# The gates of a bidirectional gated recurrence, computed as 64-row tiles with both gates of a head side by side

## The chip, the cores and the metric

One core of a Trainium2 chip runs the whole program. The metric is device time in microseconds; three runs of the kernel before give the median. Engines are named as in the profile: PE is TensorE (PEld its weight loads), ACT is ScalarE, DVE is VectorE, POOL is GpSimd, SP is SyncE, which issues the DMAs.

## The reference

A trunk of two layers over 1024 latent and 256 context tokens of width 1024. Layer 0 runs a bidirectional gated recurrence (RG-LRU) over 512 channels in 8 heads of 64 beside a spatial gating unit; layer 1 runs a short convolution beside differential attention. The change lies in the recurrence's gates. Per direction:

```python
def rglru_coeffs(xc, w_a, b_a, w_x, b_x, lam):
    xh = xc.reshape(bsz, n, LRU_HEADS, LRU_HEAD_DIM)          # 8 heads of 64
    gate_r = jax.nn.sigmoid(jnp.einsum('blhi,hij->blhj', xh, w_a).reshape(bsz, n, BRANCH_WIDTH) + b_a)
    gate_i = jax.nn.sigmoid(jnp.einsum('blhi,hij->blhj', xh, w_x).reshape(bsz, n, BRANCH_WIDTH) + b_x)
    log_a = (-LRU_C * gate_r.astype(jnp.float32)) * jax.nn.softplus(-lam.astype(jnp.float32))
    a = jnp.exp(log_a)
    bterm = jnp.sqrt(-jnp.expm1(2.0 * log_a)) * (gate_i * xc).astype(jnp.float32)
    return a, bterm
```

The gates of a head depend on that head's 64 channels alone. The scan h = a h + bterm then runs forward and backward over the tokens.

## The kernel before

Channels lie on the partitions, tokens along the free axis. The 512 channels of the recurrence are four feature blocks f of 128, two heads each; 256 context and 1024 latent tokens make 1282 columns with a gap of two. Precision comes from splitting each fp32 value into a high and a low part of a shorter format (`split`: ScalarE copies the high part, another engine subtracts), so each product is three matmuls: high by high, high by low, low by high.

Per block, `lru_x(f)` projects the channels (tile px), copies them out of PSUM on ScalarE (xp, L353 and L354), convolves them on VectorE (xl) and splits them into xh and xo. `lru_g(f)` projects the branch gate (tile pg). `lru_rec(f)` computes the recurrence's gates. For each direction d and each of the two gates g it runs nine matmuls over three chunks of columns (258, 512, 512) into a tile pgate. The two heads of a block stand as a block diagonal in a 128 x 128 weight, half of it zeros. ScalarE evicts a gate with one tanh of 128 x 1282 (L393; sigmoid is taken from tanh), to gr and gx; then tt and exp (L397, L398), products on VectorE, and in `lru_scan` a sqrt on ScalarE (L411) and the scans on VectorE. The order in the program is x(1), rec(0), scan(0), g(1), x(2), rec(1) and so on; behind rec(3) the spatial gating unit starts with the projection pz and with v (tile pv, weights wvr split into wvh on ScalarE and wvl on GpSimd).

`mod_step()` puts a piece of work of another kind, the modulation of layer 1, between the matmuls: four small matmuls in column tiles (modp), transposes (modcp) or one matmul with two outputs (gatep).

px, pg, pu, pz, pv and pgate all come from one pool of PSUM, pj, with two buffers of three banks that go round:

```python
    def pj3(name):
        t = pj.tile([128, 1536], F32, name=name, tag="pj", bufs=2)
        return t
```

TensorE's order is the program's. The order on the other engines is set by the framework's scheduler when the program is built, and each engine then runs its list in order.

Of the kernel before, what the change touches and what calls it, by code (L numbers as in the profile page):

```python
# [10 lines left out]
F32 = mybir.dt.float32  # L11
F32R = mybir.dt.float32r
# [18 lines left out]
    ("cc", 16), ("bmod0", 24), ("bmod1", 24), ("convw", 16), ("convb", 4), ("ba", 8), ("bx", 8), ("lam", 8),  # L31
# [11 lines left out]
def tile_hybrid_trunk(es: ExitStack, tc: tile.TileContext, A, out, scr=None):  # L43
# [40 lines left out]
    def P(k):  # L84
        o, w = POFF[k]
        return par[:, o:o + w]
# [11 lines left out]
    hb = const.tile([128, 16], F32, name="hb")  # L98
    V.tensor_scalar(hb[:, 0:8], P("ba"), 0.5, None, op0=ALU.mult)
    V.tensor_scalar(hb[:, 8:16], P("bx"), 0.5, None, op0=ALU.mult)  # L100
# [42 lines left out]
    def wload(src, nk=8, le=None):  # L143
        raw = wp.tile([128, nk, 128], F32, name="wraw", tag="wraw", bufs=2)
        SY.dma_start(raw, src)
        res = []
        for h in range(nk // 4):
            hi = wp.tile([128, 4, 128], F32R, name="whi", tag="whi", bufs=4)
            lo = wp.tile([128, 4, 128], F32R, name="wlo", tag="wlo", bufs=4)
            split(hi, lo, raw[:, 4 * h:4 * h + 4], le=le or G)  # L150
            res.append((hi, lo))
        return res

# [96 lines left out]
# [3 lines that stand above are left out]
# [81 lines left out]
    lru_cm = ExitStack()  # L334
    lb, ld = lru_cm.enter_context(pool("lrub")), lru_cm.enter_context(pool("lrud"))
    with pool("lrua") as lp, pool("lruc") as lc:
        def lt(name, tag, bufs, dt=F32):
            t = {"gr": lb, "gx": lb, "tt": lb, "xl": lc}.get(tag, lp).tile([128, WC], dt, name=name, tag=tag, bufs=bufs)
            return t
# [36 lines left out]
        def lru_rec(f):  # L376
            (wh, wl), = wload(A["wg"][f], nk=4)
# [3 lines left out]
            for d in range(2):  # L381
                i8 = 4 * d + f
                gts = []
                for g in range(2):
                    p = pj3("pgate")
                    m = 2 * d + g
                    for c0, n in ((0, 258), (258, 512), (770, 512)):
                        o = p[:, 254 + c0:254 + c0 + n]
                        T.matmul(o, wh[:, m], xh[:, c0:c0 + n], start=True, stop=False)
                        T.matmul(o, wh[:, m], xo[:, c0:c0 + n], start=False, stop=False)  # L390
                        T.matmul(o, wl[:, m], xh[:, c0:c0 + n], start=False, stop=True)
                    t = lt("gt", "gr" if g == 0 else "gx", 2)
                    S.activation(t, p[:, 254:1536], AF.Tanh, scale=0.5, bias=hb[:, 8 * g + i8:8 * g + i8 + 1])  # L393
                    gts.append(t)
                r, gi = gts
# [751 lines left out]
def pack(inputs):  # L1147
# [8 lines left out]
    def cols(v):  # L1156
        v = np.asarray(v)
        return v.reshape(-1, 128).T
# [6 lines left out]
        "ba": cols(a["lru_b_a"][0]), "bx": cols(a["lru_b_x"][0]), "lam": cols(a["lru_lambda"][0]),  # L1165
# [22 lines left out]
    wg = np.zeros((4, 128, 4, 128), f)  # L1188
    for fi in range(4):
        for d in range(2):  # L1190
            for g, nm in enumerate(("lru_w_a", "lru_w_x")):
                for s in range(2):
                    wg[fi, 64 * s:64 * s + 64, 2 * d + g, 64 * s:64 * s + 64] = a[nm][0, d, 2 * fi + s]
# [30 lines left out]
```

## Time and profile before

| | us |
|---|---|
| median of 3 runs | 1170.76 (1170.17 to 1171.86) |
| profiled execution, span from first to last instruction | 1170.5 |
| PE busy | 1132.6 (97%) |
| DVE busy | 738.9 (63%) |
| ACT busy | 440.2 (38%) |
| POOL busy | 329.6 (28%) |

The time of the profiled execution is its span, 1170.5 us; it lies within the three runs. Busy times are sums over the whole program, whose stages have different limits. A matmul's end is modelled, so that the time from start to start says what one costs. The recurrence's gates lie between 73 and 208 us.

### The profile page before, as it was taken

The numbers are of one execution on the slowest core, as the hardware profiler recorded it, in microseconds if no ns is written. First come the engines' busy times: TensorE is split into PE (matmuls) and PEld (weight loads), VectorE is DVE, ScalarE is ACT, GpSimd is POOL, SyncE is SP. The second block draws the span as 40 slices with busy tenths as digits, with TensorE's granted clock in tenths as the row PEclk, the third lists the DMA queues.
The fourth block names the chain that finished last, engine by engine and source line by source line (L and its number), as shares of the span: only waits on it lengthen the run. The fifth ranks groups of instructions, "written<-read, shape, count | busy, mean of one in ns | idle before, by whom it ended". The sixth has DMA issues, their size and how long they took to land.

```text
span 1170.5 us, 14967 instructions
## 1 busy us (share of the span) xinstructions
PE 1132.6 (97%) x5842; PEld 922.0 (79%) x5842; DVE 738.9 (63%) x1007; ACT 440.2 (38%) x685; POOL 329.6 (28%) x200
## 2 busy tenths in 40 slices
PE   6999999899999999999999899999999999999997
PEld 3667777678888888888887788788888788888776
DVE  5677986943411475636104668876777877738897
ACT  3453654621121234342113455544544554413110
POOL 1114212620240132258104311221121321221971
PEclk9999999999999999999999999999999999999999
DMA  9654551230332444243215411322221510126622
GB/s 373 239 182 142 180 176 41 73 130 1 120 104 71 144 139 147 96 136 140 77 45 162 113 55 54 95 76 84 77 76 37 146 62 19 46 72 249 218 99 82
DMA packets 71606, 133.93 MB, mean 114 GB/s; under 512 B 6368, under 2 KB 34912, under 8 KB 70640
## 3 DMA queue, kind: packets, MB, share of 16 engines
q1 hardware_dynamic: 71536, 132.97, 34.3%
q8 instruction: 46, 0.75, 0.3%
q14 instruction: 24, 0.20, 0.1%
HBM read 105.67 MB, written 27.28 MB: 114 GB/s over the span
## 4 chain that ended last, share of the span: by engine, by line
PE 83%; DVE 8%; DMA 3%; ACT 3%; issue 2%; POOL 0%; SPq 0%; POOLq 0%; DVEq 0%; ACTq 0%
PE px L164 5%; PE pu L164 5%; PE pg L164 5%; PE p L174 5%; PE p L175 5%; PE p L176 5%; PE pout L648 4%; PE pout L646 4%; PE pout L647 4%; PE pz L164 4%; PE psc L942 3%; PE pv L198 3%; PE pv L199 3%; PE pv L200 3%; PE psc L943 3%; PE atr L965 3%
## 5 line engine op out<-in xcount | busy, mean ns | idle before, releaser
L141 POOL TENSOR_TENSOR wlo<-wraw,whi 128x512 fp32r<-128x512 f32 x92 | 148.1, 1615 | 458.5 <-ACT whi L138 449.8
L648 PE MATMUL pout<-woh,ylo 128*128 128x512 f32 (+1 forms) x296 | 114.5, 387 | 3.1 <-DVE ylo L141 3.1
L946 ACT ACTIVATE e<-psc,st 128x1280 f32<-128x1280 f32 x64 | 85.1, 1329 | 85.6 <-DVE st L944 85.6
L646 PE MATMUL pout<-woh,yhi 128*128 128x512 f32 (+1 forms) x296 | 114.8, 388 | 0.2
L647 PE MATMUL pout<-wol,yhi 128*128 128x512 f32 (+1 forms) x296 | 114.0, 385 | 0.0
L944 DVE TENSOR_REDUCE st<-psc 128x1 f32<-128x1280 f32 x64 | 95.0, 1485 | 27.8 <-PE psc L943 27.7
L138 ACT ACTIVATE whi<-wraw 128x512 fp32r<-128x512 f32 x92 | 57.2, 628 | 134.3 <-PE p L175 27.7
L174 PE MATMUL p<-hhl,whi 128*128 128x512 f32 x256 | 106.8, 417 | 0.0
L176 PE MATMUL p<-hhl,wlo 128*128 128x512 f32 x256 | 100.7, 393 | 0.0
L175 PE MATMUL p<-hll,whi 128*128 128x512 f32 x256 | 100.5, 393 | 0.0
L942 PE MATMUL psc<-k,qh 128*128 128x512 f32 (+1 forms) x192 | 68.0, 369 | 8.4 <-ACT e L946 8.4
L943 PE MATMUL psc<-k,ql 128*128 128x512 f32 (+1 forms) x192 | 69.3, 361 | 0.0
L138 ACT ACTIVATE ah<-atr 128x512 fp32r<-128x512 f32 (+1 forms) x96 | 48.5, 525 | 51.6 <-PE atr L965 50.6
L648 PEld LDWEIGHTS pout<-woh,ylo 128*128 128x128 f32 x296 | 55.6, 188 | 15.3 <-DVE ylo L141 4.0
L646 PEld LDWEIGHTS pout<-woh,yhi 128*128 128x128 f32 x296 | 55.6, 188 | 12.1 <-DVE zt L610 0.5
L647 PEld LDWEIGHTS pout<-wol,yhi 128*128 128x128 f32 x296 | 55.7, 188 | 11.5
L138 ACT ACTIVATE yhi<-yraw 128x512 fp32r<-128x512 f32 x36 | 22.5, 630 | 103.7 <-PE pout L647 57.6
L141 DVE TENSOR_TENSOR al<-atr,ah 128x512 fp32r<-128x512 f32 (+1 forms) x96 | 55.6, 594 | 5.8 <-ACT ah L138 5.6
L176 PEld LDWEIGHTS p<-hhl,wlo 128*128 128x128 f32 x256 | 48.2, 188 | 10.7
L175 PEld LDWEIGHTS p<-hll,whi 128*128 128x128 f32 x256 | 48.6, 190 | 7.3
L141 DVE TENSOR_TENSOR ylo<-yraw,yhi 128x512 fp32r<-128x512 f32 x36 | 43.2, 1208 | 17.5 <-ACT yhi L138 17.5
L174 PEld LDWEIGHTS p<-hhl,whi 128*128 128x128 f32 x256 | 48.4, 189 | 7.2
(292 smaller groups left out, 2822.2 us busy)
## 6 DMA issues: line engine op xcount, KB each, us to landing
wraw<-in_w_in_dram SPq DMA_DIRECT2D x44, 512.0 KB, 3.7
wm<-in_w_mod_dram SPq DMA_DIRECT2D x64, 256.0 KB, 3.4
wraw<-in_w_out_dram SPq DMA_DIRECT2D x16, 512.0 KB, 3.5
wm<-in_w_mod_dram SPq DMA_DIRECT2D x7, 1024.0 KB
xt<-in_xcT_dram SPq DMA_DIRECT2D x8, 640.0 KB, 9.8
xres<-in_xc_dram SPq DMA_DIRECT2D x10, 512.0 KB, 3.7
kd<-k_d SPq DMA_DIRECT2D x16, 320.0 KB, 4.7
wvr<-in_w_v_dram SPq DMA_DIRECT2D x8, 512.0 KB, 4.4
```

What stands on the lines that cost most here:

```text
L138: S.activation(hi, src, AF.Copy)
L141: le.tensor_tensor(lo, src, f32(hi), op=ALU.subtract)
L164: T.matmul(o, wt[:, k % 4], hh[hx][:, k], start=st, stop=sp_)
L174: T.matmul(o, hi[:, k % 4], hh[:, k], start=k == 0, stop=False)
L175: T.matmul(o, hi[:, k % 4], hl_[:, k], start=False, stop=False)
L176: T.matmul(o, lo[:, k % 4], hh[:, k], start=False, stop=k == KT - 1)
L646: T.matmul(o, hi[:, i], wh[:, c], start=first and i == 0, stop=False)
L647: T.matmul(o, hi[:, i], wl[:, c], start=False, stop=False)
L648: T.matmul(o, lo[:, i], wh[:, c], start=False, stop=not first and i == 3)
L942: T.matmul(o, qh[:, m, cu], KS[m][:, c:c + n], start=True, stop=False)
L943: T.matmul(o, ql[:, m, cu], KS[m][:, c:c + n], start=False, stop=True)
L944: V.tensor_reduce(st[:, m:m + 1], p[:, 256:1536], axis=AX.X, op=ALU.max, negate=True)
```

## The change

The weights of the gates are packed anew: for each direction, head 0's 64 rows stand in the upper half and head 1's in the lower, and the 128 columns are both gates of that head (64 columns each). The block diagonal's zeros are gone, and the load is half as large (`gload`). Each matmul takes 64 rows, in the upper or the lower half of the array (`tile_position`), and the two halves' matmuls alternate. Each head has its own tile pgate, both gates in it. The tanh has to bring the lanes back into the order of the channels: four activations of 64 x 1282, one for each gate and head, in place of two of 128 x 1282. The biases are packed the same way (hg).

```diff
-    hb = const.tile([128, 16], F32, name="hb")
-    V.tensor_scalar(hb[:, 0:8], P("ba"), 0.5, None, op0=ALU.mult)
-    V.tensor_scalar(hb[:, 8:16], P("bx"), 0.5, None, op0=ALU.mult)
+    hg = const.tile([128, 16], F32, name="hg")
+    V.tensor_scalar(hg, P("bg"), 0.5, None, op0=ALU.mult)
...
+    def gload(src):
+        raw = wp.tile([128, 2, 128], F32, name="wraw", tag="wraw", bufs=2)
+        SY.dma_start(raw, src)
+        hi = wp.tile([128, 2, 128], F32R, name="whi", tag="whi", bufs=4)
+        lo = wp.tile([128, 2, 128], F32R, name="wlo", tag="wlo", bufs=4)
+        split(hi, lo, raw, le=G)
+        return (hi, lo),
...
         def lru_rec(f):
-            (wh, wl), = wload(A["wg"][f], nk=4)
+            (wh, wl), = gload(A["wg"][f])
             mod_step()
             xl, xh, xo = XL[f]
             bs = []
             for d in range(2):
                 i8 = 4 * d + f
-                gts = []
-                for g in range(2):
-                    p = pj3("pgate")
-                    m = 2 * d + g
-                    for c0, n in ((0, 258), (258, 512), (770, 512)):
-                        o = p[:, 254 + c0:254 + c0 + n]
-                        T.matmul(o, wh[:, m], xh[:, c0:c0 + n], start=True, stop=False)
-                        T.matmul(o, wh[:, m], xo[:, c0:c0 + n], start=False, stop=False)
-                        T.matmul(o, wl[:, m], xh[:, c0:c0 + n], start=False, stop=True)
-                    t = lt("gt", "gr" if g == 0 else "gx", 2)
-                    S.activation(t, p[:, 254:1536], AF.Tanh, scale=0.5, bias=hb[:, 8 * g + i8:8 * g + i8 + 1])
-                    gts.append(t)
-                r, gi = gts
+                ps = [pj3("pgate"), pj3("pgate")]
+                for c0, n in ((0, 258), (258, 512), (770, 512)):
+                    for wt, x, st, sp_ in ((wh, xh, True, False), (wh, xo, False, False), (wl, xh, False, True)):
+                        for h in range(2):
+                            r64 = slice(64 * h, 64 * h + 64)
+                            T.matmul(ps[h][:, 254 + c0:254 + c0 + n], wt[r64, d], x[r64, c0:c0 + n], start=st,
+                                     stop=sp_, tile_position=(64 * h, 0))
+                r, gi = lt("gt", "gr", 2), lt("gt", "gx", 2)
+                for g, t in enumerate((r, gi)):
+                    for h in range(2):
+                        o = slice(64 * h, 64 * h + 64)
+                        i = slice(64 * g, 64 * g + 64)
+                        S.activation(t[o], ps[h][i, 254:1536], AF.Tanh, scale=0.5,
+                                     bias=hg[i, 2 * i8 + h:2 * i8 + h + 1])
                 tt = lt("tt", "tt", 2)
```

The change moves instructions on two engines. On PE, between the two directions of block 0, the kernel before has the end of the second gate (pgate_728), the four matmuls of a mod step and the start of direction 1 (pgate_760, into a buffer whose tanh ScalarE ran first). The words in brackets are the engines and queues waited for.

```order
L391 MATMUL pgate_728<-xh_582,wlo_707 128x512
L211 MATMUL modp_755<-wm_747,csil_91 32x512 [waits DMAHW2_49]
L211 MATMUL modp_755<-wm_749,csil_91 32x512 [waits DMAHW3_49]
L211 MATMUL modp_755<-wm_751,csil_91 32x512 [waits DMAHW4_49]
L211 MATMUL modp_755<-wm_753,csil_91 32x512 [waits DMAHW5_49]
L389 MATMUL pgate_760<-xh_582,whi_706 128x258 [waits Activation_49]
L390 MATMUL pgate_760<-xo_583,whi_706 128x258
L391 MATMUL pgate_760<-xh_582,wlo_707 128x258
```

The same place on PE after the change, where pgate_761 and pgate_762 are the two heads of direction 1:

```order
L395 MATMUL pgate_716<-xh_581,wlo_706 128x512
L218 MATMUL modp_756<-wm_748,csil_91 32x512 [waits DMAHW2_49]
L218 MATMUL modp_756<-wm_750,csil_91 32x512 [waits DMAHW3_49]
L218 MATMUL modp_756<-wm_752,csil_91 32x512 [waits DMAHW4_49]
L218 MATMUL modp_756<-wm_754,csil_91 32x512 [waits DMAHW5_49]
L395 MATMUL pgate_761<-xh_581,whi_705 128x258 [waits PE_49,Activation_49]
L395 MATMUL pgate_762<-xh_581,whi_705 128x258 [waits PE_49,Activation_49]
L395 MATMUL pgate_761<-xo_582,whi_705 128x258
```

The first matmul of direction 1 and the one behind it now wait for ScalarE, one for each buffer, with the mod step as the only work ahead of them.

On ACT, around the gates of block 0, the kernel before has this order (gt is a gate, r or gi; whi belongs to the next projection's weights and xh to the next block):

```order
L393 ACTIVATE gt<-pgate,hb 128x1282
L397 ACTIVATE tt<-gt,sp 128x1282
L393 ACTIVATE gt<-pgate,hb 128x1282
L398 ACTIVATE gt<-gt,sp 128x1282
L393 ACTIVATE gt<-pgate,hb 128x1282
L138 ACTIVATE whi<-wraw 128x512
L138 ACTIVATE xh<-xl 128x1282
L393 ACTIVATE gt<-pgate,hb 128x1282
L397 ACTIVATE tt<-gt,sp 128x1282
L398 ACTIVATE gt<-gt,sp 128x1282
```

After the change the same place reads as follows; pgate_715 and pgate_716 are the heads of direction 0, gt_735 is r and gt_736 is gi.

```order
L402 ACTIVATE gt_735<-pgate_715,hg_96 64x1282
L402 ACTIVATE gt_736<-pgate_715,hg_96 64x1282
L402 ACTIVATE gt_735<-pgate_716,hg_96 64x1282
L402 ACTIVATE gt_736<-pgate_716,hg_96 64x1282
L405 ACTIVATE tt_741<-gt_735,sp_98 128x1282
L406 ACTIVATE gt_735<-gt_735,sp_98 128x1282
L137 ACTIVATE whi_934<-wraw_928 128x512
L402 ACTIVATE gt_781<-pgate_761,hg_96 64x1282
L402 ACTIVATE gt_782<-pgate_761,hg_96 64x1282
L137 ACTIVATE xh_699<-xl_694 128x1282
L402 ACTIVATE gt_781<-pgate_762,hg_96 64x1282
L402 ACTIVATE gt_782<-pgate_762,hg_96 64x1282
```

The scheduler runs both pieces of one buffer before those of the other, and tt, exp (L406) and whi now stand between the pieces of the two directions.

On ACT behind the gates of block 3, before the change, from the table load for exp to the first split of v's weights (wvh0):

```order
L398 ACT_TABLE_LOAD
L398 ACTIVATE gt_1738<-gt_1738,sp_99 128x1282
L393 ACTIVATE gt_1783<-pgate_1773,hb_96 128x1282
L393 ACTIVATE gt_1795<-pgate_1785,hb_96 128x1282
L397 ACTIVATE tt_1797<-gt_1783,sp_99 128x1282
L398 ACTIVATE gt_1783<-gt_1783,sp_99 128x1282
L411 ACT_TABLE_LOAD
L411 ACTIVATE tt_1752<-tt_1752 128x1282
L138 ACTIVATE wvh0_1829<-wvr_1827 128x512
```

And after it:

```order
L406 ACT_TABLE_LOAD
L406 ACTIVATE gt_1759<-gt_1759,sp_98 128x1282
L402 ACTIVATE gt_1806<-pgate_1786,hg_96 64x1282
L402 ACTIVATE gt_1807<-pgate_1786,hg_96 64x1282
L402 ACTIVATE gt_1806<-pgate_1787,hg_96 64x1282
L402 ACTIVATE gt_1807<-pgate_1787,hg_96 64x1282
L419 ACT_TABLE_LOAD
L419 ACTIVATE tt_1765<-tt_1765 128x1282
L405 ACT_TABLE_LOAD
L405 ACTIVATE tt_1812<-gt_1806,sp_98 128x1282
L406 ACTIVATE gt_1806<-gt_1806,sp_98 128x1282
L137 ACTIVATE wvh0_1844<-wvr_1842 128x512
```

The sqrt of direction 0 (L419) has moved ahead of tt and exp of direction 1, and a table load stands on either side of it. The same happens in the other three blocks; ACT has 14 table loads before and 22 after.

## Rows read from the trace of the kernel before

**Rows 1.** The page, the chain that ended last, by engine.

```profile
PE 83%; DVE 8%; DMA 3%; ACT 3%; issue 2%; POOL 0%; SPq 0%; POOLq 0%; DVEq 0%; ACTq 0%
```

**Rows 2.** Waits of PE from 60 to 245 us: total, times, longest.

```profile
PE pv L199 <- POOL wvl L141: 4.3, 3, 1.6
...
PE pgate L389 <- ACT gt L393: 0.2, 1, 0.2
```

**Rows 3.** Timeline of PE, block 0: start, length, instruction, count.

```profile
73.84 0.38 PE L389 MATMUL pgate<-xh,whi 128*128 128x258 f32 x1
...
75.71 0.28 PE L389 MATMUL pgate<-xh,whi 128*128 128x258 f32 x1
...
82.26 1.07 PE L211 MATMUL modp<-wm,csil 128*32 128x512 f32 x8
83.26 0.39 PE L164 MATMUL pg<-hhc,whi 128*128 128x256 f32 x1
...
86.97 1.02 PE L462 MATMUL gatep<-mb,par 128*2 128x512 f32 x2
```

**Rows 4.** Timeline of ACT, block 0 (in brackets: idle before, and its releaser).

```profile
73.34 1.02 ACT L354 ACTIVATE xp<-px 128x1024 f32<-128x1024 f32 x1
75.91 1.33 ACT L393 ACTIVATE gt<-pgate,hb 128x1282 f32<-128x1282 f32 x1 [1.54 <-PE pgate L391]
...
82.41 0.62 ACT L138 ACTIVATE whi<-wraw 128x512 fp32r<-128x512 f32 x1
82.93 1.27 ACT L138 ACTIVATE xh<-xl 128x1282 fp32r<-128x1282 f32 x1
...
85.30 1.46 ACT L397 ACTIVATE tt<-gt,sp 128x1282 f32<-128x1282 f32 x1
86.80 1.46 ACT L398 ACTIVATE gt<-gt,sp 128x1282 f32<-128x1282 f32 x1
```

**Rows 5.** Groups by line on DVE: count, busy us, mean ns, idle before.

```profile
L451 DVE COPY mb<-modp 128x512 f32<-128x512 f32 x8 | 5.5, 684 | 17.5 <-PE modp L211 17.5
...
L465 DVE TENSOR_TENSOR br<-gatep,br 2x512 f32<-2x512 f32 x4 | 2.7, 670 | 3.8 <-PE gatep L462 3.8
```

**Rows 6.** Timeline of ACT, block 3 and the split of v's weights.

```profile
205.17 1.28 ACT L398 ACT_TABLE_LOAD   x1
206.47 1.46 ACT L398 ACTIVATE gt<-gt,sp 128x1282 f32<-128x1282 f32 x1
207.83 2.54 ACT L393 ACTIVATE gt<-pgate,hb 128x1282 f32<-128x1282 f32 x2
210.26 1.46 ACT L397 ACTIVATE tt<-gt,sp 128x1282 f32<-128x1282 f32 x1
...
213.22 1.28 ACT L411 ACT_TABLE_LOAD   x1
214.52 1.28 ACT L411 ACTIVATE tt<-tt 128x1282 f32<-128x1282 f32 x1
215.70 3.22 ACT L138 ACTIVATE wvh<-wvr 128x512 fp32r<-128x512 f32 x6
```

**Rows 7.** Timeline of PE, block 3: first gate matmul, first of pz.

```profile
199.06 0.39 PE L389 MATMUL pgate<-xh,whi 128*128 128x258 f32 x1
...
209.19 0.38 PE L164 MATMUL pz<-hhc,whi 128*128 128x256 f32 x1 [0.70 <-ACT gt L393]
```

**Rows 8.** Windows of 1 us (busy per engine, granted clock, DMA) and a stall's timeline.

```profile
230.00:231.00 1.00, 0.80 (x2) 0.70 (x3) 0.96 (x2) 0.00 (x0) 1.00 (x2) 0.56 0.00 0
...
233.00:234.00 1.00, 0.47 (x2) 0.00 (x0) 1.00 (x2) 0.00 (x0) 1.00 (x1) 0.73 0.00 0
...
758.41 0.38 PE L942 MATMUL psc<-k,qh 128*128 128x256 f32 x1 [1.94 <-ACT e L946]
...
759.00:760.00 1.00, 1.00 (x4) 0.83 (x3) 1.00 (x1) 0.12 (x1) 0.00 (x0) 0.59 0.03 5
...
766.00:767.00 1.00, 1.00 (x6) 0.78 (x5) 0.00 (x0) 0.00 (x0) 0.00 (x0) 0.99 0.83 320
```

More of the change, by code (lines that the diff above doesn't have):

```diff
@@ L30 @@
 _PARAMS = [
-    ("cc", 16), ("bmod0", 24), ("bmod1", 24), ("convw", 16), ("convb", 4), ("ba", 8), ("bx", 8), ("lam", 8),
+    ("cc", 16), ("bmod0", 24), ("bmod1", 24), ("convw", 16), ("convb", 4), ("bg", 16), ("lam", 8),
     ("slng", 4), ("slnb", 4), ("lng0", 8), ("lnb0", 8), ("sconv", 12), ("subln", 1), ("sel", 2),
@@ L1164, in pack @@
         "convb": cols(a["lru_conv_b"][0]),
-        "ba": cols(a["lru_b_a"][0]), "bx": cols(a["lru_b_x"][0]), "lam": cols(a["lru_lambda"][0]),
+        "bg": np.concatenate([a[k][0].reshape(16, 64).T for k in ("lru_b_a", "lru_b_x")], 0),
+        "lam": cols(a["lru_lambda"][0]),
         "slng": cols(a["sgu_ln_g"][0]), "slnb": cols(a["sgu_ln_b"][0]),
@@ L1187, in pack @@
     r["w_out0"], r["w_out1"] = c(a["ab_w_out"][0]), c(a["cd_w_out"][0])
-    wg = np.zeros((4, 128, 4, 128), f)
+    wg = np.zeros((4, 128, 2, 128), f)
     for fi in range(4):
@@ L1192, in pack @@
                 for s in range(2):
-                    wg[fi, 64 * s:64 * s + 64, 2 * d + g, 64 * s:64 * s + 64] = a[nm][0, d, 2 * fi + s]
+                    wg[fi, 64 * s:64 * s + 64, d, 64 * g:64 * g + 64] = a[nm][0, d, 2 * fi + s]
     r["wg"] = wg
```

## The prediction

> **What bounds the kernel now.** I read the page first. The chain that ended last is TensorE for 83% of the span [rows 1]: time that TensorE loses anywhere is lost at the end, unless it waits somewhere for another engine anyway. So I went to the table of waits over the recurrence stage and what follows it (60 to 245 us). There TensorE waits for an eviction of the gates once, 0.2 us; its one larger wait is 4.3 us for wvl on GpSimd, just behind the stage [rows 2]. The stage is TensorE's: its matmuls run back to back and the other engines follow.
>
> Then the timeline of feature block 0. On TensorE [rows 3] the first gate's group starts at 73.84 and the second at 75.71, so nine matmuls take 1.87 us and the 18 of one direction 3.74. A modulation step (modp) takes 1.00, and the projection pg of the next block starts at 83.26: 9.42 us after the first gate matmul. On ScalarE [rows 4] the first tanh starts 2.07 us after its group began. What the reader is to see is the pattern: one gate is evicted while the next is computed, in the two buffers of pj, so the buffer that TensorE wants is always free.
>
> **The change, part by part.**
>
> *TensorE's own work.* 18 matmuls of 64 rows in place of 18 of 128 in each direction, the same columns. If the two halves of the array work at once, a direction takes nine slots, 1.87 us, and 8 x 1.87 = 15 us of TensorE work go. If they don't, nothing goes. The trace has no row tiles. The nearest rows are column tiles: the four of a modp step, eight records, last 1.07 us together, and one fp32 matmul of the same 512 columns, two records, 1.02 [rows 3]. So tiles side by side do run at once in this kernel; I take concurrency, and keep the serial case as a rival. The Trainium skill says the same of row tiles (TensorE: Matmul & The Clock Gate, Part 3: Packing small matmuls): matmuls in different row groups start within some 4 ns of each other. No run here shows that; by it the sum is the one below.
>
> *The tanh.* Two activations of 128 lanes become four of 64 lanes with the same 1282 columns. If an activation costs by its columns, each piece costs what a whole one does: two whole ones in a row last 2.54 us and the next starts 2.43 after their start [rows 6], so 1.215 from start to start and 1.325 for the last. If it cost by lanes, a piece would be half of that, 0.61. ScalarE has no row with fewer lanes; the nearest is VectorE, where an operation on 2 lanes takes 670 ns and one of 128 lanes, equally long, 684 [rows 5]. I take 1.215, and 0.61 as the other end. The Trainium skill (ScalarE: Activation LUTs, Step-by-step: what each stage is for) gives one element per cycle and lane, which makes lanes free and columns the price; no activation here shows it, and the sum by it is the one that I take.
>
> *The wait that this makes.* Both buffers of pj now fill at the same moment, and each is read twice. The first is free after two pieces, the second after four. TensorE's next group wants both at its first two matmuls. After direction 0 the only work in between is one mod step, so TensorE stands until the fourth piece has ended; queued behind it are a mod step and the projections, for which ScalarE's xp and VectorE's convolution wait in turn. After direction 1, pg wants one buffer, free after two pieces, but these stand on ScalarE behind tt, exp and whi of direction 0, which in the kernel before lay between the tanh. Step by step from the first gate matmul of block 0:
> - the second buffer still holds px: its copy ends at 73.34 + 1.02 = 74.36 [rows 4], and with 0.05 to TensorE's start the pairs begin 0.57 late;
> - from there to the first piece 2.07, as before;
> - four pieces 4 x 1.215 = 4.86;
> - tt, 1.50 to the start of exp [rows 4]; exp, 1.36 to an instruction that doesn't need it [rows 6]; whi, 0.52 [rows 4]: 3.38;
> - two pieces of direction 1, 1.215 + 1.325, and 0.04 until TensorE starts (pz starts at 209.19, the first of the two tanh at 207.83 ends at 209.155) [rows 6, 7]: 2.58.
> Sum 13.46 against 9.42: pg starts **4.04 us** later, with TensorE at full clock. Direction 1's matmuls are hidden here: the second buffer comes at 3 x 1.215 + 1.325 + 0.04 = 5.01 after the first piece, they are ready 2.07 later at 7.08, and ScalarE comes to them at 4.86 + 3.38 = 8.24. Blocks 1 and 2 have the same pattern; I take three times this, 12.1.
>
> *The clock.* TensorE would stand some 4 us before direction 1 (its mod step ends 1.87 + 1.00 - 2.07 = 0.8 after the first piece began, the buffer comes at 5.01) and some 3 before pg (5.01 + 1.87 + 1.00 = 7.88 against 8.24 + 2.58 = 10.82). What a stall does stands at two places [rows 8]. After the waits for wvl the granted clock fell to 0.5, which is 1.2 of 2.4 GHz, at 230.12 (0.56 in that microsecond) and rose at 233.54: 3.4 us at half. After 1.94 us of waiting at 758.41 it was at half from 759.18 to 766.02, 6.8 us, while TensorE worked. At half clock direction 1 takes 4.14 to its eviction, 5.01 + 4.14 = 9.15 against 8.24: 0.91 more per block. And 3.4 us of half clock in pg cost 1.7 (3.4 if it is 6.8 us; nothing if the clock holds). For three blocks 3 x (0.91 + 1.7) = 7.8.
>
> *The last block* ends differently. Behind its gates stand wvh on ScalarE and wvl on GpSimd, and TensorE already waits for wvl. The order shows that the sqrt of direction 0 now stands ahead of tt and exp of direction 1, with a table load on each side; over the kernel table loads go from 14 to 22. wvh begins after: 0.57 (as above), 2.07, four pieces 4.86, tt 1.50, table load 1.30, exp 1.36, four pieces 4.86, load 1.30, sqrt 1.18, load 1.30, tt 1.50, exp 1.36 [rows 4, 6], together 23.16 after 199.06 [rows 7]: 222.2 in place of 215.70, **6.5** later. TensorE itself would come 4.1 plus 1.7 of clock later, less than that, so wvl decides: 6.5.
>
> *At nothing.* The half-sized wg load and split (256 columns for 512), and one hg operation for two hb, lie on idle engines. Their cover is the projections between the gate groups; without it half a whi, 0.3 us by its row of 0.62 [rows 4], would stand on the path. VectorE gets no new work, but its chain waits longer for ScalarE; what TensorE wants of it, pg's buffer, it wants only at the next block's gates, a whole projection later.
>
> **Sum.** 12.1 + 7.8 + 6.5 = 26.4. Nothing later gives it back, as TensorE sets the end. The profiled execution's span is 1170.5 us and the median 1170.76, so they agree within 0.3; 1170.8 + 26.4 = **1197 us**.
>
> **Rivals.**
> *The halves don't work at once.* Against it stand the column tiles; for it nothing but that no row shows row tiles. Direction 0 then ends 1.87 later, and direction 1 takes 3.94 to its eviction, with 3.4 us at half clock 5.64: 10.65 against the 9.15 above, 1.5 more. Four times 3.4: 13.6 more, **1211**.
> *The clock holds.* Then only 12.1 + 6.5 are left: **1189**. Both places in rows 8 speak against it, so it lies within my forecast as its low end.
> *Faster: the pieces are cheap.* With p for a piece, the block's sum is 9.42 - 3.25 + 6p, so pg comes earlier if p is under 0.54. Then TensorE keeps a part of its 15 us. At half price, 0.61, each block still loses 0.4 and the last 1.7: **1174**. At a third of a us per piece each block gains 1.3 and the last 0.5: **1166**. Only cost by lanes without a fixed part would do this; VectorE's 2-lane row speaks against it.
>
> **How the numbers follow.** Stalls with concurrency: 0.73, from 1189 (clock holds) to 1203 (6.8 us of half clock each time: 12.1 + 3 x 4.3 + 7.5 = 32.5). Serial halves: 0.20, around 1211. Cheap pieces: 0.06, of which 0.03 faster and 0.02 within 0.2%. The rest is what I don't see. The range from 1188 to 1212 leaves out the cheap pieces and the slow part of the serial case. A change of 0.2%, 2.3 us, is about what a measurement of this kernel can tell from none. Faster 0.03, same 0.02, slower 0.95.
>
> **What would show it.** A tanh piece of 64 lanes near 1.3 us, 32 of them. TensorE waiting for L402 some 3 to 4 us before each direction 1 and 1 to 3 before each pg and before pz. Starts of the two halves' matmuls paired, a direction in 1.9 us (3.7 if serial). Half clock behind the stalls. wvh 6 to 7 us later against block 3's first gate matmul. The prediction is wrong if pieces take much under 1.2 us, or if the stage's stalls are there and the end comes no later.

## The result, and the profile after

The changed kernel takes **1198.85 us** (median of 4 runs, 1197.59 to 1200.02) against 1171.31 of the kernel before beside it (4 runs): ratio 1.0229, 95% interval 1.0216 to 1.0241. It is slower by some 27 us.

TensorE's waits from 60 to 275 us, in total, times and longest, in the changed kernel:

```profile
PE pgate L395 <- ACT gt L402: 16.2, 8, 2.3
PE pg L171 <- ACT gt L402: 5.9, 3, 2.2
PE pv L206 <- POOL wvl L140: 4.8, 4, 2.2
PE pz L171 <- ACT gt L402: 2.4, 1, 2.4
PE pv L205 <- DVE zt L531: 1.9, 1, 1.9
PE pgate L395 <- ACT xp L361: 0.2, 1, 0.2
```

The reader compares it with [rows 2]: waits for a tanh of the gates were 0.9 us (0.2 at pgate, 0.7 at pz [rows 7]) and are 24.5 us now, at each gate group and behind it. In the chain that ended last, ScalarE's share has doubled, GpSimd's has come up from nothing and TensorE's has fallen against [rows 1]:

```profile
PE 74%; DVE 8%; ACT 6%; DMA 4%; POOL 4%; issue 3%; SPq 0%; POOLq 0%; DVEq 0%; ACTq 0%
```

TensorE's timeline of block 0, which answers to [rows 3]:

```profile
75.61 0.38 PE L395 MATMUL pgate<-xh,whi 64*128 64x258 f32 x1
76.18 0.39 PE L395 MATMUL pgate<-xh,whi 64*128 64x258 f32 x1 [0.19 <-ACT xp L361]
...
76.53 0.52 PE L395 MATMUL pgate<-xh,whi 64*128 64x512 f32 x2
76.76 0.51 PE L395 MATMUL pgate<-xo,whi 64*128 64x512 f32 x2
77.00 0.51 PE L395 MATMUL pgate<-xh,wlo 64*128 64x512 f32 x2
...
78.13 1.06 PE L218 MATMUL modp<-wm,csil 128*32 128x512 f32 x8
80.86 0.42 PE L395 MATMUL pgate<-xh,whi 64*128 64x258 f32 x1 [1.66 <-ACT gt L402]
83.56 0.58 PE L395 MATMUL pgate<-xh,whi 64*128 64x258 f32 x1 [2.28 <-ACT gt L402]
...
84.16 0.84 PE L395 MATMUL pgate<-xh,whi 64*128 64x512 f32 x2
84.58 0.84 PE L395 MATMUL pgate<-xo,whi 64*128 64x512 f32 x2
...
87.06 1.45 PE L218 MATMUL modp<-wm,csil 128*32 128x512 f32 x8
90.17 0.38 PE L171 MATMUL pg<-hhc,whi 128*128 128x256 f32 x1 [1.66 <-ACT gt L402]
```

A pair of matmuls of 512 columns, one in each half, starts every 0.235 us, as one full-array matmul did in the kernel before: the halves work at once, and a direction takes half the slots. (A row of two lasts 0.51 because the second of a pair starts some 0.12 behind the first.) Then TensorE stands 1.66 us for the first buffer and 2.28 for the second, works through direction 1 at half clock (0.43 for a pair), and stands again before pg: 14.56 us from the first gate matmul to pg, where [rows 3] has 9.42.

ScalarE in the same block, which answers to [rows 4]:

```profile
78.12 5.38 ACT L402 ACTIVATE gt<-pgate,hg 64x1282 f32<-64x1282 f32 x4 [2.00 <-PE pgate L395]
83.53 1.46 ACT L405 ACTIVATE tt<-gt,sp 128x1282 f32<-128x1282 f32 x1
85.02 1.46 ACT L406 ACTIVATE gt<-gt,sp 128x1282 f32<-128x1282 f32 x1
86.80 0.63 ACT L137 ACTIVATE whi<-wraw 128x512 fp32r<-128x512 f32 x1 [0.32 <-PE pgate L395]
87.45 2.66 ACT L402 ACTIVATE gt<-pgate,hg 64x1282 f32<-64x1282 f32 x2
```

Four pieces last 5.38 us, so a piece of 64 lanes costs 1.345 from start to start, more than a whole one of 128 lanes (1.215 by [rows 6]). whi doesn't run on behind exp: it waits for direction 1's matmuls.

The granted clock in that stretch (windows of 1 us: length, TensorE's busy time, clock, DMA share and GB/s), which answers to [rows 8]:

```profile
80.00:81.00 1.00, 0.14 (x1) 1.00 0.57 168
81.00:82.00 1.00, 0.28 (x1) 0.53 0.98 358
...
86.00:87.00 1.00, 1.00 (x6) 0.50 0.00 0
87.00:88.00 1.00, 1.00 (x9) 0.56 0.00 0
88.00:89.00 1.00, 0.51 (x8) 1.00 0.00 0
```

Half clock, 1.2 of 2.4 GHz, begins during the second wait and lasts 6.8 us, over all of direction 1. The last block, ScalarE, answers to [rows 6]:

```profile
237.41 1.28 ACT L419 ACT_TABLE_LOAD   x1
238.71 1.28 ACT L419 ACTIVATE tt<-tt 128x1282 f32<-128x1282 f32 x1
240.00 1.28 ACT L405 ACT_TABLE_LOAD   x1
241.30 1.46 ACT L405 ACTIVATE tt<-gt,sp 128x1282 f32<-128x1282 f32 x1
242.79 1.46 ACT L406 ACTIVATE gt<-gt,sp 128x1282 f32<-128x1282 f32 x1
244.16 3.21 ACT L137 ACTIVATE wvh<-wvr 128x512 fp32r<-128x512 f32 x6
```

Where the 27.7 us between the two spans (1198.2 and 1170.5) lie, from the timelines of both kernels: the first gate matmul comes 1.77 later (75.61 against 73.84); the gate groups of blocks 0 to 2, from their first matmul to the next projection, take 14.56, 14.43 and 14.44 in place of 9.42, 8.72 and 9.12, 16.2 in all; the projections behind them 33.19, 34.77 and 33.04 in place of 33.18, 33.22 and 31.56, 3.0; block 3 to pz 14.71 in place of 10.13, 4.6; pz to v's first matmul 15.61 in place of 14.11, 1.5. Together 27.1; the other 0.6 lies behind.

The first of these terms lies ahead of the gates, at the start of the program. In the kernel before, two matmuls of 512 columns take 0.62 us from the first pg on; in the changed kernel they take 1.05, as at half clock, until 22.3 us. Below, the first rows show this, and the second rows, the same matmul in both kernels, come 1.79 apart (TensorE's timeline of the kernel before, then of the changed one):

```profile
19.68 0.62 PE L164 MATMUL pg<-hhl,whi 128*128 128x512 f32 x2
...
22.41 0.38 PE L164 MATMUL px<-hhc,whi 128*128 128x256 f32 x1
```

```profile
20.18 1.05 PE L171 MATMUL pg<-hhl,whi 128*128 128x512 f32 x2
...
24.20 0.38 PE L171 MATMUL px<-hhc,whi 128*128 128x256 f32 x1
```

So 1.8 of the 27.7 us is the time at which full clock came in these two executions. It goes with neither kernel: the last version below has the kernel before's matmuls, and its gates begin at 75.55; one with halves at once begins them at 74.02. Whether the change makes a late rise likelier isn't shown.

### The profile page after: what moved, and what is told of

Read it like the earlier page. It is cut to its first block, busy times and chain, and to the rows that moved or that the text cites. A ratio compares the mean times of both kernels' runs of the same rounds, so it can differ in the third digit from the quotient of the medians.

```text
span 1198.2 us, 15003 instructions
## 1 busy us (share of the span) xinstructions
PE 1135.1 (95%) x5842; PEld 922.6 (77%) x5842; DVE 738.6 (62%) x1006; ACT 473.2 (39%) x709; POOL 311.3 (26%) x200
## 4 chain that ended last, share of the span: by engine, by line
PE 74%; DVE 8%; ACT 6%; DMA 4%; POOL 4%; issue 3%; SPq 0%; POOLq 0%; DVEq 0%; ACTq 0%
PE pg L171 5%; PE pu L171 5%; PE px L171 4%; PE p L181 4%; PE p L182 4%; PE p L183 4%; PE pz L171 4%; PE pv L205 3%; PE psc L950 3%; PE pv L207 3%; PE pv L206 3%; PE psc L951 3%; PE pout L656 3%; PE pout L655 3%; PE pout L654 3%
## 5 line engine op out<-in xcount | busy, mean ns | idle before, releaser
L140 POOL TENSOR_TENSOR wlo<-wraw,whi 128x512 fp32r<-128x512 f32 (+1 forms) x92 | 132.0, 1439 | 495.4 <-ACT whi L137 478.9
L952 DVE TENSOR_REDUCE st<-psc 128x1 f32<-128x1280 f32 x64 | 95.0, 1484 | 27.7 <-PE psc L951 27.6
L137 ACT ACTIVATE whi<-wraw 128x512 fp32r<-128x512 f32 (+1 forms) x92 | 56.4, 619 | 127.5 <-PE p L182 28.2
```

What stands on the lines that cost most here:

```text
L137: S.activation(hi, src, AF.Copy)
L140: le.tensor_tensor(lo, src, f32(hi), op=ALU.subtract)
L952: V.tensor_reduce(st[:, m:m + 1], p[:, 256:1536], axis=AX.X, op=ALU.max, negate=True)
```

## The experiments

One number says most of each version: the time from a block's first gate matmul to the first of the next projection, by the timeline of TensorE.

| version | block 0, 1, 2, 3 (us) | time (us) | ratio to the kernel before, 95% interval |
|---|---|---|---|
| kernel before | 9.42, 8.72, 9.12, 10.13 | 1171.3 | |
| halves at once, whole tanh (lanes mixed) | 9.69, 9.58, 9.59, 10.28 | 1177.35 | 1.0037 (1.0024 to 1.0050) |
| before, tanh in pieces | 11.66, 11.67, 11.68, 11.64 | 1183.48 | 1.0089 (1.0069 to 1.0108) |
| before, both gates at once | 11.87, 11.78, 11.79, 11.84 | 1183.11 | 1.0096 (1.0074 to 1.0118) |
| changed, one half after the other | 11.74, 11.64, 12.86, 11.64 | 1188.55 | 1.0141 (1.0124 to 1.0158) |
| changed, tt and exp in pieces instead | 12.64, 12.53, 12.53, 13.37 | 1194.34 | 1.0183 (1.0155 to 1.0211) |
| changed, TensorE kept busy | 14.15, 14.03, 14.04, 14.74 | 1196.74 | 1.0204 (1.0181 to 1.0227) |
| changed | 14.56, 14.43, 14.44, 14.71 | 1198.85 | 1.0229 (1.0216 to 1.0241) |
| before, both gates at once, pieces | 17.66, 17.57, 17.93, 18.19 | 1207.51 | 1.0293 (1.0277 to 1.0308) |

**One half after the other.** The loop over the halves is moved outside:

```diff
-                for c0, n in ((0, 258), (258, 512), (770, 512)):
-                    for wt, x, st, sp_ in (...):
-                        for h in range(2):
-                            r64 = slice(64 * h, 64 * h + 64)
+                for h in range(2):
+                    r64 = slice(64 * h, 64 * h + 64)
+                    for c0, n in ((0, 258), (258, 512), (770, 512)):
+                        for wt, x, st, sp_ in (...):
```

> The kernel after, with the two halves' matmuls one after the other: the nine of the upper half, then the nine of the lower, so nothing works at once and each direction costs TensorE 3.7 us again. If the loss is the wait for the eviction of two buffers that fill at the same moment (my theory), this must be faster than the kernel after although TensorE works longer: the first buffer is ready 1.9 us earlier than the second, its two pieces of 1.345 us run meanwhile, and the scheduler's order puts two pieces of direction 1 ahead of exp and whi. From the first gate matmul of block 0: 2.07 + 4 pieces 5.38 + tt 1.5 + 2 pieces 2.7 = 11.7 to pg, 2.3 us over the kernel before; blocks 1 and 2 alike, 2.6 to 3.0; the last block 5.8 by wvh. Sum some 14 us: 1185 us, between 1181 and 1191. If the loss came from the row tiles themselves (changing the array's form, slower loads) or if TensorE's work were what counts, it would be no faster than the kernel after: 1199 us, or 15 more, 1213.

1188.55 us, 10 less than the changed kernel. The nine matmuls of a half need its own buffer alone: in block 0 direction 1's first half starts at 80.47, when the first buffer is free, and fills while direction 0's second is evicted; its pieces start at 84.62, where the changed kernel has 87.45. Waits for the gates' tanh at pgate fall from 16.2 to 6.4 us. (The halves are not wholly apart in this version: in direction 0 the lower half starts before the upper half's last three matmuls, as shown at the end.)

**Pieces alone.** The kernel before, its full-array matmuls and their order kept, each tanh cut in two on its own lanes:

```diff
-                    S.activation(t, p[:, 254:1536], AF.Tanh, scale=0.5, bias=hb[:, 8 * g + i8:8 * g + i8 + 1])
+                    for h in range(2):
+                        q = slice(64 * h, 64 * h + 64)
+                        S.activation(t[q], p[q, 254:1536], AF.Tanh, scale=0.5,
+                                     bias=hb[q, 8 * g + i8:8 * g + i8 + 1])
```

> The kernel before with one thing of the change alone: each tanh of 128 lanes written as two of 64 lanes, each on its own lanes; the matmuls stay whole. If the pieces alone make the loss, the order on ScalarE is that of the serial case and so is the sum: some 14 us over the kernel before, 1185 us (1181 to 1190), with TensorE waiting for ScalarE ahead of each direction 1 and each pg. If the row tiles make the loss, this stays within 2 us of the kernel before, 1171. A piece on its own lanes that overlaps the next as whole ones do would take 1.215 from start to start, one that doesn't 1.345 as in the kernel after; the sum then differs by some 3 us.

1183.48 us: two more activations per direction cost some 11 us where the gates still take turns. The pieces cost what they cost in the changed kernel, whose group stands second here (by line: busy us, mean ns, idle before):

```profile
L395 ACT ACTIVATE gt<-pgate,hb 64x1282 f32<-64x1282 f32 x32 | 42.5, 1328 | 7.1 <-PE pgate L391 6.6
```

```profile
L402 ACT ACTIVATE gt<-pgate,hg 64x1282 f32<-64x1282 f32 x32 | 42.4, 1326 | 8.6 <-PE pgate L395 8.0
```

So it isn't writing to other lanes that makes a piece dear.

**Whole tanh.** The changed kernel, two activations of 128 lanes per direction:

```diff
-                    for h in range(2):
-                        ...
-                        S.activation(t[o], ps[h][i, 254:1536], AF.Tanh, scale=0.5,
-                                     bias=hg[i, 2 * i8 + h:2 * i8 + h + 1])
+                    S.activation(t, ps[g][:, 254:1536], AF.Tanh, scale=0.5, bias=hg[:, 2 * i8 + g:2 * i8 + g + 1])
```

> The kernel after with two whole tanh of 128 lanes in each direction, one for each buffer, in place of four pieces: the lanes are not brought back into the order of the channels, so the gates are mixed up and the output is not the reference's; the amount of work behind is the same. It keeps the halves at once and takes the pieces away. By my sum: 0.57 + 2.07 + 2.43 + tt, exp and whi 3.4 + one tanh 1.3 = 9.8 to pg of block 0, 0.4 us over the kernel before; blocks 1 and 2 0.6 to 1.0; the last 0.4; with a clock that falls in the shorter stalls at times 0 to 5 more: 1174 us, between 1170 and 1178, so no gain although 15 us of TensorE's work are gone. If TensorE's work is what counts once the pieces are away, 1156.

1177.35 us, at the upper end of what was expected: without the pieces some 22 of the 27 us are gone. But the kernel is not faster than before either, though TensorE has half the gate slots: in block 0 it still waits 0.3, 0.8 and 1.6 us for ScalarE. The groups are 1.8 us longer than before in all; in the profiled execution 2.2 more lie ahead of the gates, where the clock was at half for longer, 1.6 in a projection that met half clock, and as much behind pz.

**TensorE kept busy.** The changed kernel with matmuls that nothing reads, in the stalls:

```diff
                 mod_step()
+                dm = psb("dum")
+                for _ in range((14, 10)[d]):
+                    T.matmul(dm, hhl[:, 0, 0:128], hhl[:, 0, 0:512], start=True, stop=True)
```

> The kernel after with matmuls put into the two waits, 14 ahead of direction 1 and 10 ahead of the next projection (128 x 512, of the modulated input, into a spare PSUM tile that nobody reads), to hold TensorE's clock; they last 3.3 and 2.4 us, less than the waits at full clock. If half clock behind the waits costs what the trace of the kernel after shows (1.5 us in pg of blocks 1 and 2, a late whi in block 0, part of pz), the time falls by some 4 us: 1195, between 1192 and 1197, and the granted clock stays at 1.0 through the four blocks. If the clock costs nothing there, 1199; if the extra matmuls get in the way, above 1200.

1196.74 us. The granted clock is 1.00 in each window from 80 to 92 us of block 0; the two late projections are back at 33.23 and 31.53 us, and the group of each of the first three blocks is 0.4 shorter. So TensorE reaches v at 245.32 in place of 250.36. But half of that goes again in v, where it waits 3.1 us for VectorE's zt in place of 1.9: rsum, behind v's first three tiles, starts at 275.10 in place of 277.61. By the times the clock's share is 2.1 us, and the two intervals overlap.

**What halves at once are worth in this order.** The kernel before with the two gates' full-array matmuls alternating, so that both buffers fill together; first with whole tanh, then with the pieces:

```diff
+                ps = [pj3("pgate"), pj3("pgate")]
+                for c0, n in ((0, 258), (258, 512), (770, 512)):
+                    for wt, x, st, sp_ in (...):
+                        for g in range(2):
+                            T.matmul(ps[g][:, 254 + c0:254 + c0 + n], wt[:, 2 * d + g], x[:, c0:c0 + n], start=st, stop=sp_)
```

> The kernel before (full-array tiles, one gate per group, whole tanh), with one thing changed: the matmuls of both gates alternate, so that the two buffers fill together, as the changed kernel's do, but at 18 slots of TensorE per direction instead of nine. From the rows measured so far, after a block's first gate matmul: first tanh 0.57 + 3.94 = 4.5, two whole tanh 2.5, direction 1's matmuls 3.9 at full clock, whi 0.6 (its buffer comes free when these matmuls end), one tanh 1.3, so the next tile starts 12.9 later where the kernel before has 9.1 and the changed kernel with whole tanh 9.6; up to 14.4 with direction 1 at half clock. If halves at once are worth their slots inside this order (mine): 3 blocks x 3.8 to 5.3, some 2 of clock in pg, some 6 at the last block, 1190 us (1185 to 1197). If the loss came from the order of filling alone and the concurrency were worth nothing where TensorE waits: the time of the version with whole tanh and halves at once, 1177 us.

1183.11 us, just under the expected range: the first tanh came 4.05 after the first gate matmul, not 4.5, and TensorE kept its full clock. Against whole tanh with halves at once it is 5.8 us slower, not the 15 of the saved slots (by the groups alone 8.1).

```diff
-                    S.activation(t, p[:, 254:1536], AF.Tanh, scale=0.5, bias=hb[:, 8 * g + i8:8 * g + i8 + 1])
+                    for h in range(2):
+                        q = slice(64 * h, 64 * h + 64)
+                        S.activation(t[q], p[q, 254:1536], AF.Tanh, scale=0.5,
+                                     bias=hb[q, 8 * g + i8:8 * g + i8 + 1])
```

> The same with each tanh in two pieces of 64 lanes on their own lanes: the changed kernel in everything but that its matmuls take the whole array, 18 slots per direction. It is the price that the rival of serial halves put at 1211 us. From the rows measured so far: first piece 4.5 after the first gate matmul, four pieces 5.4, direction 1's matmuls 3.9 (7.5 at half clock), whi 0.6, two pieces 2.7, so the next tile starts 17.2 to 20 later where the changed kernel has 14.5. Three blocks x 2.7 to 5.5 and about 3 at the last one above the changed kernel's 1199: 1211 us (1206 to 1218). If concurrency is worth nothing in this order: 1199 us, as the changed kernel.

1207.51 us, in the range; 8.7 above the changed kernel. Its four groups are 13.2 longer; 2.5 are won back in the projections and 1.5 behind pz, which stay at full clock here, and 1.7 at the start of the program.

**What stands in the queue.** tt and exp made to wait for direction 1's last piece, by a bias that is made from it (times zero):

```diff
+                V.tensor_scalar(ga[:, 0:1], gs[1][1][:, 0:1], 0.0, sp2[:, i8:i8 + 1], op0=ALU.mult, op1=ALU.add)
-                S.activation(tt, r, AF.Tanh, scale=sp2[:, i8:i8 + 1], bias=sp2[:, i8:i8 + 1])
+                S.activation(tt, r, AF.Tanh, scale=sp2[:, i8:i8 + 1], bias=ga[:, 0:1])
```

> The changed kernel with the same results, but the bias of tt is made from a column of direction 1's second gate, so that ScalarE can't begin tt and exp before all eight pieces are done: the 2.9 us of tt and exp leave the queue ahead of direction 1's pieces. By my prediction's sum they were 2.9 us of the path in each block: three times 2.9 and the last block's, so 1188 us. By the trace of the changed kernel they hide behind direction 1's matmuls at half clock (whi, next in the queue, waited for these matmuls to end): the next tile comes as late as before, and the time stays at 1198 us (1195 to 1200).

1205.20 us (ratio 1.0278, 1.0259 to 1.0297), outside both expectations, but the groups answer the question: 14.56, 14.11, 14.42 and 13.87. In block 0 nothing is won, and in blocks 1 and 2 no more than 0.3, for ScalarE now stands idle until direction 1's matmuls are through (its timeline in block 0):

```profile
78.52 5.36 ACT L402 ACTIVATE gt<-pgate,hg 64x1282 f32<-64x1282 f32 x4 [2.01 <-PE pgate L395]
87.17 0.63 ACT L137 ACTIVATE whi<-wraw 128x512 fp32r<-128x512 f32 x1 [3.29 <-PE pgate L395]
```

Up to pz the two kernels are level (234.84 and 234.75 us). The loss comes behind: the last sps matmul of the gating unit starts at 341.45 in place of 336.58, and in that stage TensorE waits 2.5 us for VectorE's vf, which it doesn't in the changed kernel, and it has half clock for 13.7 us from 255.9 on, where the changed kernel has 6.8. The chain that ended last runs over VectorE's last products of block 3, until 272.0, then over a store and a transfer of weights to ScalarE's split and vf. So the later tt and exp pushing VectorE's chain back is the likely reason; it wasn't tried by itself.

The same with the fillers:

```diff
                 mod_step()
+                dm = psb("dum")
+                for _ in range((14, 10)[d]):
+                    T.matmul(dm, hhl[:, 0, 0:128], hhl[:, 0, 0:512], start=True, stop=True)
```

> The run before this one with the filler matmuls behind the mod steps, which kept TensorE at full clock. Now direction 1's matmuls take 2.1 to their eviction in place of some 3.5, so what stands on ScalarE ahead of direction 1's pieces counts again as far as it is longer than that: four pieces 2.5 + 5.4, matmuls 2.1, whi 0.6, two pieces 2.7, 13.4 after the first gate matmul, where the version with the fillers alone has 14.1. Three times 0.7 and about as much at the last block below that version's 1196.7: 1194 us (1190 to 1197). If tt and exp are worth their whole 2.9 us: 1186.

1194.01 us (1.0179, 1.0162 to 1.0196), as expected: groups 13.30, 13.09, 13.21, 13.06. With TensorE at full clock, the 2.9 us of tt and exp cost 0.8 to 0.9 in each of the first three blocks; at half clock they hide but for 0.0 to 0.3.

**The lanes put right later.** tanh whole, tt and exp in pieces of 64 lanes, the columns of one half swapped in the weights so that VectorE finds its lanes in place:

```diff
+                for h in range(2):
+                    S.activation(ts[h], ps[h][:, 254:1536], AF.Tanh, scale=0.5, bias=hg[:, 2 * i8 + h:2 * i8 + h + 1])
...
+                for t, c, fn in ((tt, sp2, AF.Tanh), (ex, sn4, AF.Exp)):
+                    for h in range(2):
+                        o, i = slice(64 * h, 64 * h + 64), slice(64 - 64 * h, 128 - 64 * h)
+                        S.activation(t[o], ts[h][i], fn, scale=c[i, i8:i8 + 1], bias=c[i, i8:i8 + 1])
```

> Halves at once, and the same results as the changed kernel, but the lanes are put right one step later: the gates' tanh are whole (two per direction, which free the buffers), and tt and exp are the ones in two pieces of 64 lanes, four pieces per direction as before in all. If what costs is how long ScalarE takes to free the two buffers, counting all that stands in its queue ahead of it: after the first gate matmul the first tanh at 2.6, two whole ones 2.45, four pieces of tt and exp at about 1.48 = 5.9, whi 0.6, one tanh 1.3, so the next tile starts 12.9 later (changed kernel 14.5, whole tanh with lanes mixed 9.6): about 1.6 x 3 less than the changed kernel's 1199 and the same last block: 1194 us (1188 to 1197). If instead a piece costs only because it stands between a buffer and TensorE's next group, direction 0's wait is two activations shorter and the pieces behind it are free: 1178 us, as the version with mixed lanes.

1194.34 us, as the first theory had it: what stands ahead in ScalarE's queue counts, not only what reads the buffer. It also settles a rival: this version has 14 table loads, as many as the kernel before, where the changed kernel has 22, and it still loses 23 us. The extra table loads are not what makes most of the loss.

Both together: whole tanh, and tt and exp of blocks 0 to 2 behind those of direction 1.

```diff
+                if f < 3:
+                    for n, c in ((0, sp2), (1, sn4)):
+                        V.tensor_scalar(sp[:, 2 * d + n, i8:i8 + 1], gs[1][1][:, 0:1], 0.0, c[:, i8:i8 + 1],
+                                        op0=ALU.mult, op1=ALU.add)
...
-                        S.activation(t[o], ts[h][i], fn, scale=c[i, i8:i8 + 1], bias=c[i, i8:i8 + 1])
+                        S.activation(t[o], ts[h][i], fn, scale=c[i, i8:i8 + 1], bias=(sp[:, 2 * d + n] if f < 3 else c)[i, i8:i8 + 1])
```

> The run before this one with tt and exp of blocks 0 to 2 made to wait for direction 1's tanh (biases made from a column of its second tile), so that nothing but whi stands between the four whole tanh of a block; block 3 as in the run before. After the first gate matmul: first tanh 2.6, two whole ones 2.45, direction 1's matmuls 2.1 at full clock, whi 0.6, one tanh 1.3: the next tile starts 9.1 later, as in the kernel before (9.1), with half of TensorE's gate slots: three blocks at nothing. The last block as in the run before, wvh some 23 after its first gate matmul where the kernel before has 16.6: 6.5 late; and up to 2 at the start of the program. 1179 us (1173 to 1183). If the pieces, wherever they stand, cost their 1.35 each in the end because ScalarE falls behind: as the run before this one.

1183.30 us (1.0098, 1.0071 to 1.0124), at the upper edge; groups 8.90, 12.28, 10.71, 13.36. Block 0 is as forecast (9.1) and shorter than in the kernel before (9.42). In block 1 TensorE meets another wait, on VectorE, which copies a modulation tile only behind the convolution (timelines of TensorE and of VectorE):

```profile
127.89 0.85 PE L225 MATMUL modcp<-ident,mb 128*128 128x128 f32 x4 [4.75 <-DVE mb L474]
```

```profile
121.62 5.62 DVE L366 SCALAR_TENSOR_TENSOR xl<-xp,par,xl 128x1282 f32<-128x1282 f32 x3
127.15 0.68 DVE L474 COPY mb<-modp 128x512 f32<-128x512 f32 x1
```

The time won on ScalarE's path is spent there waiting for VectorE; what makes block 2 longer wasn't looked into. No version beats the kernel before.

**Why pieces don't overlap.** The version with pieces alone, each cut again at column 641, so that two of the same lanes follow each other:

```diff
+                        for c in (0, 641):
+                            S.activation(t[q, c:c + 641], p[q, 254 + c:895 + c], AF.Tanh, scale=0.5,
+                                         bias=hb[q, 8 * g + i8:8 * g + i8 + 1])
```

> The version with the kernel before's gates and each tanh in two pieces of 64 lanes, with each piece cut once more, into two of 641 columns, the two of the same lanes one behind the other. By the rows so far such a piece lasts about 0.80 us (1.326 for 1282 columns less 641 at 0.82 ns, from the copies of 256 and 1024 columns, 0.39 and 1.02). If successive activations overlap by some 0.1 us unless the second reads other lanes than the first: four pieces in a row 3.0 to 3.1 us, two overlaps. If 64-lane activations never overlap: 3.2 to 3.3. If it is only by chance that four of 1282 columns didn't: 2.9. The time is looked at once: some 2.2 us more on ScalarE per block than the version with two pieces, 1185 to 1195 us.

1187.03 us in one run. The group of pieces, and four in a row on ScalarE's timeline:

```profile
L396 ACT ACTIVATE gt<-pgate,hb 64x641 f32<-64x641 f32 x64 | 47.2, 786 | 4.5 <-PE pgate L391 4.0
```

```profile
85.08 2.96 ACT L396 ACTIVATE gt<-pgate,hb 64x641 f32<-64x641 f32 x4
```

4 x 0.786 is 3.14; without overlap and with gaps of 0.02 it would be 3.20, with three overlaps of 0.11 it would be 2.81. 2.96 is two overlaps. The expectation, which took 0.80 for a piece, had 3.0 to 3.1 for this and 2.9 for chance, and 2.96 lies between; the single starts decide. The second of two on the same lanes starts 0.69 to 0.70 us behind the first, before that one's 0.79 are over, and the first on the other lanes 0.79 to 0.81, when they are. That holds in every row of pieces in this trace.

## Why the prediction was right, point by point

The direction and the place were right, and the size within 2 us, but some of that is luck: terms that were wrong cancel. The terms:

- **Concurrency**: right. Pairs start 0.235 us apart, so the serial rival falls. The Trainium skill has matmuls of different row groups start some 4 ns apart (TensorE: Matmul & The Clock Gate, Part 3: Packing small matmuls); the trace agrees for direction 0's chunk of 258 columns, where the two of a pair start 1 to 4 ns apart, and differs behind it, where it is 0.11 to 0.12 us. The rival's price was right for the groups, 13.2 us in the version with full-array tiles in the same order where the rival had 13.6; in the time it was 8.7, 1207.5 and not 1211.
- **The pieces**: priced at 1.215, measured 1.345. By columns, not lanes, as said, but four in a row don't overlap: 5.41 to the start of tt where the sum has 4.86.
- **Behind them** the sum has 3.38 for tt, exp and whi, or direction 1's matmuls if these are later. They were later, as it forecast for half clock, but whi waits for them as well and runs after them: direction 1's first piece started 9.33 after the first piece of direction 0 (87.45 less 78.12), where the sum has 9.15 with half clock. So the queue of tt and exp, which the sum without the clock counts in full, costs next to nothing here and 0.9 at full clock, as the two runs on the order show.
- **A block** was to lose 4.04 and 0.91 of clock, 4.95. It lost 5.14, 5.71 and 5.32 (16.2 in all, the sum has 14.8). Most of what is over lies in the kernel before: the sum takes block 0's 9.42 three times, but blocks 1 and 2 take 8.72 and 9.12 there, 1.0 less. The groups themselves came within 0.2 of the sum's 13.46 + 0.91 = 14.37, because two errors cancel: at full clock, in the version kept busy, a group takes 14.03 to 14.15, 0.6 to 0.7 over the sum (the pieces' missing overlap), and half clock adds 0.4, not 0.91.
- **The clock behind the stall**: 1.7 in each pg, 5.1 in all. Measured 0.0, 1.55 and 1.48: in block 0 the clock was back at 88 us, before pg began. This term was too large by 2.1.
- **The last block**: 6.5 by wvh. wvh began 24.1 us after the first gate matmul in place of 16.6, 7.5 later, again by eight pieces of 0.13 more; TensorE reached v 6.1 later. But wvl doesn't decide, as the prediction has it. Behind the waits for wvl TensorE waits for zt, which frees pz's buffer and stands on VectorE behind the scans; the chain that ended last runs over it in both kernels (TensorE's timeline of the kernel before, then of the changed one):

```profile
236.71 0.61 PE L198 MATMUL pv<-wvh,hhc 128*128 128x512 f32 x1 [0.95 <-DVE zt L523]
```

```profile
264.35 0.80 PE L205 MATMUL pv<-wvh,hhc 128*128 128x512 f32 x1 [1.95 <-DVE zt L531]
```

From block 3's first gate matmul that is 44.31 us in place of 37.65, 6.7 later. So VectorE's chain, which the prediction put at nothing, sets the end of the last block, and the number came out near all the same. With whole tanh wvh comes on time (16.8), and this wait still ends 1.6 later than before.
- **Not foreseen**: the gates began 1.8 us later, by the clock at the start of the program. As far as the runs show this is chance of the two profiled executions.

The terms that were too small (1.4 in the groups, 1.8 at the start) and too large (2.1 in the clock) cancel in part: 26.4 forecast, 27.5 measured.

Where the 15 us of saved slots went: the order that fills both buffers at once takes the alternation of filling and evicting away. With full-array tiles and whole tanh that alone costs some 10 us; halves at once give 6 back, and the rest of the 15 is spent waiting for ScalarE. The pieces, 22 us in this order and 11 in the order of before, make the loss what it is.

## What to carry to other kernels

Before packing matmuls side by side, look at what empties their outputs: with two buffers, tiles that fill at once can't be evicted in turn, and the time won on TensorE becomes a wait for the evicting engine. An activation cost by its columns here, so splitting one by lanes doubled it (1.33 us for 64 lanes as for 128). Price a group by the evicting engine's whole queue, and then ask which of its entries would have waited for the matmuls anyway.

## What the hardware showed that was not expected

- Successive activations on ScalarE overlap by about 0.11 us when they use the same lanes and the second doesn't overwrite what the first reads, and not when the second reads other lanes: whole ones start 1.215 apart at a length of 1.325 [rows 6], pieces on changing lanes 1.345; exp, which overwrites the tile that tt reads, starts 1.49 behind tt's start at a length of 1.46. The Trainium skill (ScalarE: Activation LUTs, What ACT_TABLE_LOAD costs) has successive activations overlap by some 93 ns, without these conditions; the trace agrees for the same lanes alone.
- Halves of the array run at once even where their matmuls are not issued in turn. In the version with one half after the other, the second half's first matmul started at 76.62, when the first half had its last three still to start; the last row is one of these (TensorE's timeline):

```profile
76.61 0.39 PE L395 MATMUL pgate<-xh,wlo 64*128 64x512 f32 x1
76.62 0.38 PE L395 MATMUL pgate<-xh,whi 64*128 64x258 f32 x1
76.84 0.28 PE L395 MATMUL pgate<-xo,whi 64*128 64x258 f32 x1
76.84 0.40 PE L395 MATMUL pgate<-xh,whi 64*128 64x512 f32 x1
```

- Waits of 0.3, 0.8 and 1.6 us in block 0, with whole tanh, left the granted clock at 1.00 from 80 to 90 us; in the changed kernel it fell at 81.1 us, in the second of two waits of 1.66 and 2.28 us, and stayed at half for 6.8 us. In block 1 of the version with whole tanh the clock fell too, from 130 to 133 us within pg, behind a wait of 1.96 us ahead of pg (1.56 in blocks 0 and 2, where it held); whether that wait made it fall wasn't settled.
